# Expert buffers on early-dying tiles, the expert sort behind the first unit, and a product taken by rows, in a two-block transformer kernel

## The chip, the cores and the metric

One core of a Trainium2 chip runs the whole program. The metric is the device time of one launch in microseconds (us); 1440.97 us is the median of three runs of the kernel before.

## The reference

Two residual blocks follow each other on a sequence of 256 tokens of width 1024, all in float32.

- First block: `x + gate1 * mixer(h)`, then `x + gate2 * moe(h)`, and an RMS norm. `h` is an RMS norm of `x`, scaled and shifted by a modulation vector computed from the condition `c` (1024 x 6144 weights, "ada"). The mixer joins a 31-tap causal convolution branch and a chunked linear-attention branch (mLSTM) and ends in a 1024 x 1024 product with `w_out`.
- The MoE picks for each token one of 4 groups, then the best 2 of the 8 experts in that group. Each of the 32 experts is a gated product: `(silu(x Wg) * (x Wu)) Wd`, with 1024 x 512, 1024 x 512 and 512 x 1024 weights, 6 MB an expert, 192 MB in all. The two outputs of a token are added with their routing weights.
- Second block: two layers of differential attention and of grouped-query attention, each with a gated feed-forward of width 2816 and its own modulation.

## The kernel before

**Tiles and engines.** Weights come in as 1 MB tiles `raw` (128 x 2048 float32) through one DMA queue, that of SP, in a fixed order. In the mixer and the second block a weight is split into a high and a low part (`hi` on ACT, `lo` on DVE) and multiplied three times; in the MoE it is multiplied as it is. The tile framework places semaphores and orders each engine's instructions: of those that are ready in its plan, the one written earliest goes first. On the chip each engine then runs its list in that order and waits where it must. `issue_after(ins)` adds to this that what is written in its block, on the engine of `ins`, is issued behind `ins`.

**Space.** Pools lie behind each other in the order in which they are opened, and a closed pool's space goes to the next one opened. The mixer's pools `pha` (its activations), `worka` (`gtmp`, `adarow`, `junk`) and `hia` (split weights) are closed at its end. Then the MoE opens `moe` (its own tiles), `raw2` (3 weight tiles) and `raw3` (5), on the same space. The 8 tiles of `rawp` live through the whole kernel. An expert load waits until every older tile under its buffer is finished with.

**Between mixer and MoE.** `second` multiplies 512 columns of `w_out` for both halves `t` of 128 tokens; `add_gated` adds the product to `x` and `sq_part` squares it (tile `junk`); `norm_rows` makes `xn`, transposes it (`nt`), and `modulated` makes `h32`, of which 16 pieces of 128 x 128 are needed. From it come the 36 routing logits (`plg`), a chain of small DVE instructions from `lg` (L756) to `a01` (L796), and the rank of each token within its expert (`prk`, `sl` L813). `xh` and `xl` are the two parts of `xn`. Modulation work for a later layer stands in a list `queue`, from which `fill` runs steps: 8 loads with their products (`ada`), and a last step that uses the row (`adac`).

**Sort.** `counts` (`cnt`) adds up the tokens of each expert, `place` and `perm` rank the experts, `rows` gives their `order`, and `pst`, `psp`, `swp` bring slots and weights into that order. The first four experts are fixed; the others run in the order found, and `SP` reads `order` before it issues their loads. All of it stands ahead of the first gather.

**Units.** Ten units of 2 or 4 experts: `gather` (every second unit) builds selection matrices `gr` and multiplies them with `xl` and `xh` into `xg`; `gate_up` multiplies `xg` with the weights (`pg`, `pu`) into `hid`; `scatter_of` transposes `gr` (`pG`); `transposed` makes `hT`; `down` multiplies (`pd`), and the unit's `combine` adds into `acc` after the next unit's gate and up. Expert loads are numbered 0 to 191 and rotate over 16 buffers, so load 16 goes where load 0 was: unit 0 has loads 0 to 11. Buffers alternate:

```python
pools["raw"], pools["n"] = [raw2, rawp] * 3 + [raw3, rawp] * 5, 0
```

Ahead of unit 2 stands `fallback`, code for experts with too many tokens: a branch (L853) that every engine meets and that these inputs jump over. After the MoE, `late`, `workb`, `hib` and `xn` are opened on the MoE's space, `rot` and `gqk` are loaded, and the second block begins with `x + acc`, two norms (DVE and ACT) and the first `dense` product.

Of the kernel before, what the change touches and what calls it, by code (L numbers as in the profile page):

```python
# [42 lines left out]
def kernel(ctx: ExitStack, tc: tile.TileContext, I, cst, out):  # L43
# [156 lines left out]
    def ada_steps(key, w, ccol, b0, nb, use):  # L200
# [6 lines left out]
        def step(i):  # L207
            def f():
# [159 lines left out]
    def second(H, w, n0, name, fills=1, kn=KT, n=512):  # L368
        ps = [pa(name) for _ in range(2)]
        for kh in range(kn // 4):  # L370
            wt = split(load_k(w, kh * 4, 4, n0, n))
            for t in range(2):
                for kk in range(4):
                    k = kh * 4 + kk
                    mm3(ps[t][:, :n], (H[0][:, k, t * 128:(t + 1) * 128], H[1][:, k, t * 128:(t + 1) * 128]),
                        wt(kk, 0, n), k == 0, k == kn - 1)
        fill(fills)
        return ps
# [7 lines left out]

    pp = pha.enter_context(tc.tile_pool(name="pha", bufs=1))
# [30 lines left out]
    ca = pp.tile([128, C_PA - C_P], F32, name="ca")  # L418
    SP.dma_start(out=ca, in_=cst[:, C_P:C_PA])
    SP.dma_start(out=bif, in_=I["b_if"].rearrange("o n -> n o"))  # L420
    wif = pp.tile([128, KT, 8], F32, name="wif")
# [8 lines left out]
    wdc = pp.tile([128, 124], F32, name="wdc")  # L430
# [5 lines left out]
    ifg = pp.tile([128, 2, 8], F32, name="ifg")  # L436

    def gates_a():
        wifh = pp.tile([128, KT, 8], F32R, name="wifh")
        ACT.activation(wifh, wif, AF.Copy)  # L440
        wifl = pp.tile([128, KT, 8], F32R, name="wifl")
# [4 lines left out]
        ifr = pp.tile([8, T], F32, name="ifr", tag="ifr")  # L446
# [6 lines left out]
    def gates_b():  # L453
        li, fg = ifg[:, :, 0:4], ifg[:, :, 4:8]
        af = pp.tile([128, 2, 4], F32, name="af")
# [3 lines left out]
        lf = pp.tile([128, 2, 4], F32, name="lf")  # L459
# [5 lines left out]
        bt = pp.tile([128, 2, 4], F32, name="bt")  # L465
        DVE.tensor_copy(bt, pbt)
        rt = pp.tile([128, 2, 4], F32, name="rt")
# [3 lines left out]
    def gates_c(rt, bt):  # L471
# [3 lines left out]
        mx = [pp.tile([4, 128 + T], F32, name=f"mx{i}") for i in range(2)]  # L475
# [11 lines left out]
        en = pp.tile([128, 2, 4], F32, name="en")  # L487
# [24 lines left out]
    lp = pp.tile([64, 2], F32, name="lp")  # L512
# [5 lines left out]
    ls = pp.tile([128, 2], F32, name="ls")  # L518
# [13 lines left out]
    va = pp.tile([128, 2, NH, 129], F32, name="va")  # L532
# [4 lines left out]
    so = pp.tile([128, 2, 512], F32, name="so", tag="so")  # L537
# [4 lines left out]
    mrh = pp.tile([4, T], F32R, name="mrh", tag="ifr")  # L542
    DVE.tensor_copy(mrh, mrow)
    mrl = pp.tile([4, T], F32R, name="mrl")
    sub_lo(mrl, mrow, mrh)
    sel4r = pp.tile([4, 4, 128], F32R, name="sel4r")
    DVE.tensor_copy(sel4r, sel4)
    identr = pp.tile([128, 128], F32R, name="identr")
    DVE.tensor_copy(identr, ident)
    maskr = pp.tile([128, 128], F32R, name="maskr")  # L550
    DVE.tensor_copy(maskr, maskt)
    hm = pp.tile([128, 2, NH, 128], F32, name="hm")
    nums = {}
    for h in range(NH):
# [5 lines left out]
        wT = pp.tile([128, 384], F32, name="wT", bufs=2)  # L560
# [22 lines left out]
    st = pp.tile([128, 8, 6], F32, name="st")  # L583
    mv = pp.tile([128, 8, 2], F32, name="mv")
# [3 lines left out]
    rs = pp.tile([128, 8], F32, name="rs")  # L588
# [45 lines left out]
    sq = pp.tile([128, 4, T], F32, name="sq", tag="so")  # L634
# [43 lines left out]
    for n in range(2):  # L678
        ps = second(M, I["w_out"][0], 512 * n, "wo", 0)
        wo.append(ps)  # L680
# [3 lines left out]
    fill(len(queue))  # L684
# [4 lines left out]
    with tc.tile_pool(name="moe", bufs=1) as pp, \  # L689
            tc.tile_pool(name="raw2", bufs=3) as raw2, tc.tile_pool(name="raw3", bufs=5) as raw3:  # L690
        pools["raw"], pools["n"] = [raw2, rawp] * 3 + [raw3, rawp] * 5, 0
# [3 lines left out]
        def expert_loads():  # L695
            for ne, r0 in UNITS:
                w = ewt[r0] = [{}, {}, {}]
                for r in range(r0, r0 + ne):
                    if r not in at:
                        at[r] = nc.values_load(order[0:1, r:r + 1], engines=[mybir.EngineType.SP], min_val=0, max_val=NE - 1,  # L700
                                               skip_runtime_bounds_check_because="a permutation of the experts")
# [32 lines left out]
        for _ in modulated(nt, AB2, lambda ks, ts: h32[:, ks, ts]):  # L734
            pass
# [3 lines left out]
        for t in range(2):  # L739
            for k in range(KT):  # L740
                mm(plg[:, t, :], h32[:, k, t * 128:(t + 1) * 128], wr[:, k, :], k == 0, k == KT - 1)
        for t in range(2):
            DVE.tensor_copy(xh[:, t, :], xn[:, t, :])
            sub_lo(xl[:, t, :], xn[:, t, :], xh[:, t, :])
# [62 lines left out]
        counts = pc("cnt")  # L807
        for t in range(2):
            mm(counts[0:64, 0:32], ones[:, 0:64], a01[:, t, :], t == 0, t == 1)
        for d in range(2):  # L810
            for t in range(2):
                mm(counts[32 * d:32 * d + 32, 32:33], a01[:, t, :], ones[:, 0:1], t == 0, t == 1)
        DVE.scalar_tensor_tensor(sl, prk, 1.0, a01, op0=ALU.add, op1=ALU.mult)  # L813


        scratch2 = pp.tile([128, 512], F32, name="scratch2", tag="yl", bufs=2)
        kb = tl([64, 33], "kb")
        DVE.tensor_tensor(kb, counts[0:64, 0:33], km[0:64, 0:33], ALU.add)
        cnt = tl([64, 1], "cnt")
        DVE.tensor_copy(cnt, counts[0:64, 32:33])  # L820
        above = tl([64, 32], "above")
        DVE.tensor_scalar(above, kb[:, 0:32], kb[:, 32:33], None, op0=ALU.is_gt)
        place = pp.tile([64, 1], F32, name="place")
        DVE.tensor_reduce(place, above, axis=AX, op=ALU.add)
        perm = scratch2[0:64, 0:64]
        DVE.tensor_scalar(perm, iota[0:64], place, km[0:64, 34:35], op0=ALU.subtract, op1=ALU.is_equal)
        rows = pb("rows")
        mm(rows[0:1, 0:32], km[0:32, 33:34], perm[0:32, 0:32])
        mm(rows[0:1, 32:64], cnt[0:32], perm[0:32, 0:32])
        order = pp.tile([1, 32], I32, name="order")  # L830
        DVE.tensor_copy(order, rows[0:1, 0:32])
        excess = scratch2[0:1, 320:352]
        DVE.tensor_tensor(excess, rows[0:1, 32:64], km[0:1, 35:67], ALU.subtract)
        mx1 = tl([1, 1], "mx1")
        DVE.tensor_reduce(mx1, excess, axis=AX, op=ALU.max)
        ovi = pp.tile([1, 1], I32, name="ovi")
        DVE.tensor_scalar(ovi, mx1, 0.5, None, op0=ALU.is_gt)
        pst = pb("pst")
        for t in range(2):
            PE.transpose(pst[0:64, t * 128:(t + 1) * 128], sw[:, t, :], ident)  # L840
        swT = scratch2[0:64, 64:320]
        DVE.tensor_copy(swT, pst[0:64, 0:256])
        psp = pb("psp")
        for t in range(2):
            mm(psp[:, t * 64:(t + 1) * 64], swT[:, t * 128:(t + 1) * 128], perm)
        swp = pp.tile([128, 2, 64], F32, name="swp")
        DVE.tensor_copy(swp, psp[:, 0:128].rearrange("p (t n) -> p t n", t=2))
        slp, wEp = swp[:, :, 0:32], swp[:, :, 32:64]

        def fallback():  # L850
            over = nc.values_load(ovi, min_val=0, max_val=1,
                                  skip_runtime_bounds_check_because="a comparison gives zero or one")
            with tc.If(over > 0, preferred_fallthrough_block=False):  # L853
                wide = pp.tile([64, 33], F32, name="wide")
                DVE.tensor_scalar(wide[:, 32:33], place, WIDE - 0.5, float(CAP4), op0=ALU.is_lt, op1=ALU.mult)
# [37 lines left out]
        def gather(u):  # L893

            ne, r0 = UNITS[u]
            cap = 128 // ne
            src = sl if r0 < FIXED else slp
            gr = pp.tile([128, 2, 256], F32R, name="gr", bufs=2)
            for t in range(2):
                DVE.tensor_tensor(gr[:, t].rearrange("p (e s) -> p e s", s=cap),  # L900
                                  iota[:, None, 0:cap].to_broadcast([128, 2 * ne, cap]),
                                  src[:, t, r0:r0 + 2 * ne].unsqueeze(2).to_broadcast([128, 2 * ne, cap]), ALU.is_equal)
            xg = pp.tile([128, KT, 256], F32, name="xg", tag="xg", bufs=2)
            for k2 in range(KT // 2):
                ps = pb("gath")
                for j in range(2):
                    k = 2 * k2 + j
                    o = ps[:, j * 256:(j + 1) * 256]
                    for t in range(2):
                        mm(o, xl[:, t, k * 128:(k + 1) * 128], gr[:, t, :], t == 0, False)  # L910
                        mm(o, xh[:, t, k * 128:(k + 1) * 128], gr[:, t, :], False, t == 1)
# [533 lines left out]
```

## Time and profile before

| | |
|---|---|
| median of 3 runs | 1440.97 us (1440.58 to 1442.58) |
| the profiled execution's own time | 1442.87 us |
| its span, first to last instruction | 1441.1 us |
| mean granted TensorE clock | 0.965 |
| busy share of the span | PE 90%, DVE 43%, ACT 34%, POOL 4% |

The span is cut into four parts by eye: start and mixer to about 261 us, routing to about 290 us, the units to about 746 us, and the second block. Times in rows are us from the span's start. PE is TensorE, PEld its weight loads, DVE VectorE, ACT ScalarE, POOL GpSimd, SP SyncE; a q behind a name is the engine's sequencer. A PE product of float32 operands shows as two instructions.

### The profile page before, as it was taken

How to read it: one execution, taken by the hardware profiler on the slowest of the kernel's cores; microseconds unless marked ns; L12 is line 12 of the kernel's file. 1: busy time of each engine (PE TensorE's matmuls, PEld its weight loads, DVE VectorE, ACT ScalarE, POOL GpSimd, SP SyncE). 2: the span in 40 equal slices, each digit the busy share in tenths (PEclk: the TensorE clock that was granted, in tenths of full speed). 3: DMA queues.
4: the chain of work that ended last, by engine and by line, in shares of the span. 5: the costliest groups of instructions: out<-in, count | busy, mean ns of one | idle time of the engine just before them, and what ended most of it. 6: DMA issues, size and time to landing. Idle time of an engine off the chain costs nothing.

```text
span 1441.1 us, 20075 instructions
## 1 busy us (share of the span) xinstructions
PE 1292.9 (90%) x8125; PEld 889.5 (62%) x8125; DVE 620.7 (43%) x1074; ACT 491.0 (34%) x840; POOL 58.0 (4%) x99
## 2 busy tenths in 40 slices
PE   5799999897997777677769999999999999999997
PEld 1686897644342222121117876698999777799997
DVE  0799857511111011010026545754444764744454
ACT  1465354311010000010025645643442554644442
POOL 0000000000000000000002220000000120000000
PEclk9899999798999999899998999999999999999999
DMA  8987557798899999999989666757554665855500
GB/s 303 403 287 258 196 193 264 305 415 374 375 426 425 426 425 426 426 426 425 426 347 366 225 216 224 261 185 273 172 194 144 223 226 195 297 185 176 175 30 30
DMA packets 142658, 408.83 MB, mean 284 GB/s; under 512 B 10057, under 2 KB 90430, under 8 KB 111842
## 3 DMA queue, kind: packets, MB, share of 16 engines
q1 hardware_dynamic: 142562, 407.51, 74.2%
q8 instruction: 65, 1.06, 0.3%
q14 instruction: 31, 0.25, 0.0%
HBM read 406.43 MB, written 1.05 MB: 283 GB/s over the span
## 4 chain that ended last, share of the span: by engine, by line
PE 67%; DMA 25%; DVE 3%; issue 2%; ACT 1%; POOL 1%; SPq 0%; POOLq 0%; DVEq 0%; ACTq 0%
DMA raw<-experts_dram 23%; PE ada L124 6%; PE fg L120 3%; PE fu L119 3%; PE fg L119 3%; PE fg L121 3%; PE fu L120 3%; PE fu L121 3%; PE facc L119 3%; PE facc L120 3%; PE facc L121 3%; PE pd L124 2%; PE dense L119 2%; PE dense L120 2%; PE dense L121 2%; PE pu L124 2%
## 5 line engine op out<-in xcount | busy, mean ns | idle before, releaser
L92 DVE TENSOR_TENSOR lo<-raw,hi 128x1024 fp32r<-128x1024 f32 x120 | 145.2, 1230 | 127.3 <-ACT hi L90 125.0
L110 DVE TENSOR_TENSOR lo<-raw,hi 128x1024 fp32r<-128x1024 f32 x120 | 146.2, 1224 | 95.6 <-ACT hi L108 95.3
L90 ACT ACTIVATE hi<-raw 128x1024 fp32r<-128x1024 f32 x120 | 125.1, 1061 | 145.0 <-PE facc L121 79.1
L108 ACT ACTIVATE hi<-raw 128x1024 fp32r<-128x1024 f32 x120 | 125.9, 1057 | 122.3 <-issue 55.8
L124 PE MATMUL pu<-raw,xg 128*32 128x512 f32 (+1 forms) x512 | 108.7, 638 | 29.8 <-DMA raw<-experts_dram 29.8
L124 PE MATMUL pg<-raw,xg 128*32 128x512 f32 (+1 forms) x512 | 117.5, 690 | 17.5 <-DMA raw<-experts_dram 17.5
L124 PE MATMUL pd<-raw,hT 128*32 128x512 f32 (+1 forms) x512 | 113.5, 597 | 16.0 <-DMA raw<-experts_dram 8.3
L124 PE MATMUL ada<-raw,cc 128*32 128x512 f32 x576 | 98.6, 638 | 7.2 <-DMA raw<-in_w_ada_dram 6.4
L928 DVE TENSOR_TENSOR hid<-hid,pu 128x256 f32<-128x256 f32 x20 | 7.5, 418 | 226.1 <-PE pu L124 226.1
L119 PE MATMUL fg<-Hh,lo 128*128 128x256 f32 x352 | 100.7, 286 | 4.3 <-DVE Hh L351 4.3
L120 PE MATMUL fg<-Hl,hi 128*128 128x256 f32 x352 | 100.8, 286 | 0.9 <-DVE Hl L115 0.9
L121 PE MATMUL fg<-Hh,hi 128*128 128x256 f32 x352 | 100.5, 286 | 0.0
L119 PE MATMUL fu<-Hh,lo 128*128 128x256 f32 x352 | 100.5, 285 | 0.0
L120 PE MATMUL fu<-Hl,hi 128*128 128x256 f32 x352 | 100.0, 284 | 0.0
L121 PE MATMUL fu<-Hh,hi 128*128 128x256 f32 x352 | 99.9, 284 | 0.0
L124 PEld LDWEIGHTS pu<-raw,xg 128*32 128x32 f32 (+1 forms) x512 | 28.2, 123 | 98.5 <-DMA raw<-experts_dram 53.7
L124 PEld LDWEIGHTS pd<-raw,hT 128*32 128x32 f32 (+1 forms) x512 | 31.1, 116 | 84.6 <-issue 58.5
L119 PE MATMUL dense<-hi,Hl 128*128 128x256 f32 x288 | 82.9, 288 | 0.0
L120 PE MATMUL dense<-lo,Hh 128*128 128x256 f32 x288 | 81.5, 283 | 0.0
L121 PE MATMUL dense<-hi,Hh 128*128 128x256 f32 x288 | 81.4, 284 | 0.0
L124 PEld LDWEIGHTS pg<-raw,xg 128*32 128x32 f32 (+1 forms) x512 | 28.1, 129 | 82.4 <-issue 46.5
L966 DVE SCALAR_TENSOR_TENSOR pd<-pd,ws,gate 128x512 f32<-128x512 f32 x20 | 15.2, 759 | 133.1 <-PE pd L124 132.1
(413 smaller groups left out, 2665.1 us busy)
## 6 DMA issues: line engine op xcount, KB each, us to landing
raw<-experts_dram SPq DMA_DIRECT2D x192, 1024.0 KB
raw<-in_ada_w_dram SPq DMA_DIRECT2D x48, 1024.0 KB
raw<-in_f_w_in_dram SPq DMA_DIRECT2D x44, 1024.0 KB
raw<-in_w_ada_dram SPq DMA_DIRECT2D x24, 1024.0 KB
raw<-in_f_w_out_dram SPq DMA_DIRECT2D x22, 1024.0 KB
raw<-in_w_in_dram SPq DMA_DIRECT2D x20, 1024.0 KB
raw<-in_a_w_qkv_dram SPq DMA_DIRECT2D x12, 1024.0 KB
raw<-in_b_w_qkv_dram SPq DMA_DIRECT2D x6, 1024.0 KB
```

The costliest lines, as they stand in the source:

```text
L90: ACT.activation(hv, src, AF.Copy)
L92: DVE.tensor_tensor(lv, src, hv.bitcast(F32), ALU.subtract)
L108: ACT.activation(hv, src, AF.Copy)
L110: DVE.tensor_tensor(lv, src, hv.bitcast(F32), ALU.subtract)
L119: PE.matmul(o, al, bh, start=first, stop=False, skip_group_check=True)
L120: PE.matmul(o, ah, bl, start=False, stop=False, skip_group_check=True)
L121: PE.matmul(o, ah, bh, start=False, stop=last, skip_group_check=True)
L124: return PE.matmul(o, a, b, start=first, stop=last, skip_group_check=True)
L928: DVE.tensor_tensor(hid[:, c], hid[:, c], pgu[1][:, c], ALU.mult)
L966: DVE.scalar_tensor_tensor(pd, pd, ws, gate2[:, n * 512:(n + 1) * 512], op0=ALU.mult, op1=ALU.mult)
```

## The change

- The mixer's tiles are divided into `p1` (`pha1`: 28.5 KB a partition, all that is finished with before the last products) and `pp` (`pha`: `upad`/`ah`, `t8` for `sga` and `sgb`, `uacc`/`al`, 33.5 KB). `p1` is opened first. The MoE opens `raw2` and `raw3` first and `moe` behind them, and the ring of 16 becomes 3 of `raw2`, 2 of `rawp`, 5 of `raw3`, 6 of `rawp`.
- The last `w_out` product runs all of token half 0 first, then half 1.
- Of `h32`, DVE makes the upper four pieces of both halves (before: of half 1 alone). `xh` and `xl` are queued behind DVE's last piece.
- The modulation row's last step (`adarow`, `adac`) is one step `end`; that of the next layer is issued behind the last logit product, followed by three products that nothing reads (`warm`).
- The first gather stands right behind `sl`. The sort becomes a function, whose PE work is queued behind the last `up` product of unit 0, together with that unit's `scatter_of`; loads 24 to 27 are written behind it.

```diff
-                if i == n - 1:
-                    st["a"] = pools["work"].tile([128, 512], F32, name="adarow")
-                    ACT.copy(st["a"], ps)
             return f
-        return [step(i) for i in range(n)] + [lambda: use(st["a"])]
+        def end():
+            a = pools["work"].tile([128, 512], F32, name="adarow", **pools.get("adarow", {}))
+            ACT.copy(a, st["ps"])
+            use(a)
+        return [step(i) for i in range(n)] + [end]
...
-    def modulated(banks, AB, dst):
+    def modulated(banks, AB, dst, share=lambda ks, ts: ks.start and ts.start):
...
-                if ks.start and ts.start:
-                    DVE.tensor_scalar(d[:, j, :], src, A, B, op0=ALU.mult, op1=ALU.add)
+                if share(ks, ts):
+                    chain["mod"] = DVE.tensor_scalar(d[:, j, :], src, A, B, op0=ALU.mult, op1=ALU.add).ins
...
+        for kh, t in ((0, 0), (1, 0), (0, 1), (1, 1)) if rows_first else ((0, 0), (0, 1), (1, 0), (1, 1)):
+            if kh not in wts:
+                wts[kh] = split(load_k(w, kh * 4, 4, n0, 512))
...
+    p1 = pha.enter_context(tc.tile_pool(name="pha1", bufs=1))
     pp = pha.enter_context(tc.tile_pool(name="pha", bufs=1))
...
-        ps = second(M, I["w_out"][0], 512 * n, "wo", 0)
+        ps = second(M, I["w_out"][0], 512 * n, "wo", 0, n == 1)
...
-    fill(len(queue))
+    fill(len(queue) - 1)
...
-    with tc.tile_pool(name="moe", bufs=1) as pp, \
-            tc.tile_pool(name="raw2", bufs=3) as raw2, tc.tile_pool(name="raw3", bufs=5) as raw3:
-        pools["raw"], pools["n"] = [raw2, rawp] * 3 + [raw3, rawp] * 5, 0
+    with tc.tile_pool(name="raw2", bufs=3) as raw2, tc.tile_pool(name="raw3", bufs=5) as raw3, \
+            tc.tile_pool(name="moe", bufs=1) as pp:
+        pools["raw"], pools["n"] = [raw2] * 3 + [rawp] * 2 + [raw3] * 5 + [rawp] * 6, 0
...
-        for _ in modulated(nt, AB2, lambda ks, ts: h32[:, ks, ts]):
+        for _ in modulated(nt, AB2, lambda ks, ts: h32[:, ks, ts], lambda ks, ts: ks.start):
             pass
...
-        for t in range(2):
-            DVE.tensor_copy(xh[:, t, :], xn[:, t, :])
-            sub_lo(xl[:, t, :], xn[:, t, :], xh[:, t, :])
+        with tc.issue_after(end.ins):
+            pools["work"], pools["adarow"] = pp, {"tag": "yh", "bufs": 2}
+            fill(len(queue))
+            pools.pop("adarow")
+            warm = pc("warm")
+            for _ in range(3):
+                mm(warm, ones, cs[:, 0:512])
+        with tc.issue_after(chain["mod"]):
+            for t in range(2):
+                DVE.tensor_copy(xh[:, t, :], xn[:, t, :])
+                sub_lo(xl[:, t, :], xn[:, t, :], xh[:, t, :])
...
+        gathered = gather(0)
+        def sort():
+            counts = pc("cnt")
...
-            load_to(done + RAW_BUFS + RAW2_BUFS)
+            load_to(24 if u == 0 else done + RAW_BUFS + RAW2_BUFS)
             if u % 2 == 0:
-                gr, xg = gather(u)
+                gr, xg, _ = gather(u) if u else gathered
...
-            gT, ws = scatter_of(ne, r0, gr[:, :, g])
+            with tc.issue_after(chain["up"]) if u == 0 else nullcontext():
+                if u == 0:
+                    sort()
+                    load_to(done + RAW_BUFS + RAW2_BUFS)
+                gT, ws = scatter_of(ne, r0, gr[:, :, g])
```

## Rows read from the trace of the kernel before

**Rows 1.** The page's busy times: us (share of the span) xinstructions.

```profile
PE 1292.9 (90%) x8125; PEld 889.5 (62%) x8125; DVE 620.7 (43%) x1074; ACT 491.0 (34%) x840; POOL 58.0 (4%) x99
```

**Rows 2.** Busy time by stretch: length, engines' busy us (instructions), PE clock, DMA share, GB/s.

```profile
240.00:264.00 24.00, 24.00 (x122) 17.38 (x120) 12.45 (x17) 8.10 (x13) 0.93 (x1) 1.00 0.52 188
...
356.00:364.00 8.00, 8.00 (x39) 4.35 (x40) 0.76 (x2) 2.89 (x6) 0.00 (x0) 0.87 0.07 24
364.00:742.00 378.00, 297.17 (x1520) 93.46 (x1516) 37.71 (x84) 26.79 (x54) 0.00 (x0) 0.95 1.01 425
```

**Rows 3.** Timeline, expert loads issued by SP: start, us, instruction; loads 4 to 19; 16; 40.

```profile
262.02 37.26 SPq L69 DMA_DIRECT2D raw<-experts_dram  x16
...
294.67 0.33 SPq L69 DMA_DIRECT2D raw<-experts_dram  x1
...
362.91 0.34 SPq L69 DMA_DIRECT2D raw<-experts_dram  x1
```

**Rows 4.** Timeline from the mixer's last sum to the first gather.

```profile
261.61 0.69 DVE L383 TENSOR_TENSOR x<-x,gtmp 128x512 f32<-128x512 f32 x1
...
264.82 1.46 POOL L309 TENSOR_TENSOR rstd<-ms,half 128x1 f32<-128x1 f32 x1 [2.12 <-DVE ms L314]
...
271.52 0.23 DVE L756 TENSOR_TENSOR scratch<-plg,brt 128x72 f32<-128x72 f32 x1 [1.17 <-PE plg L124]
...
276.22 0.42 PE L124 MATMUL prk<-scratch,cs 128*128 128x32 f32 x1 [4.74 <-DVE scratch L796]
...
277.63 0.64 PE L124 MATMUL cnt<-scratch,ones 128*64 128x32 f32 x4
277.74 0.23 DVE L813 SCALAR_TENSOR_TENSOR sw<-prk,scratch 128x64 f32<-128x64 f32 x1 [0.84 <-PE prk L124]
...
278.82 0.41 DVE L900 TENSOR_TENSOR gr<-cs,sw 128x256 fp32r<-128x256 f32 x1
...
283.15 1.12 PE L124 MATMUL psp<-scratch 64*128 64x64 f32 x4
...
284.20 0.58 PE L124 MATMUL gath<-gr,xl 128*128 128x256 f32 x1
```

**Rows 5.** Groups on DVE, 260.7 to 272 us: count, busy us, mean ns.

```profile
L115 DVE TENSOR_TENSOR xl<-xn,xh 128x1024 fp32r<-128x1024 f32 x2 | 2.4, 1220 | 0.0
L743 DVE CAST xh<-xn 128x1024 fp32r<-128x1024 f32 x2 | 1.4, 690 | 1.6 <-ACT xn L322 1.6
L342 DVE TENSOR_SCALAR h<-nt,AB 128x128 f32<-128x128 f32 x4 | 1.4, 402 | 0.0
L324 DVE TENSOR_SCALAR xn<-x,rstd 128x1024 f32<-128x1024 f32 x1 | 0.8, 753 | 0.4 <-POOL rstd L309 0.4
```

**Rows 6.** Stretches of 4 us around the gather; the third number from the right is PE's clock.

```profile
272.00:276.00 4.00, 0.00 (x0) 0.00 (x0) 3.62 (x21) 0.98 (x5) 0.00 (x0) 0.59 1.01 422
...
288.00:292.00 4.00, 4.00 (x20) 2.82 (x21) 0.06 (x1) 2.28 (x6) 0.00 (x0) 0.78 1.01 426
```

**Rows 7.** Timeline of PE between the first unit's up and down products.

```profile
304.33 1.45 PE L124 MATMUL pu<-raw,xg 128*64 128x512 f32 x4
...
308.25 0.65 PE L124 MATMUL pd<-raw,hT 128*64 128x512 f32 x2 [0.83 <-issue]
```

**Rows 8.** The branch over the fallback: count, ns least/median/most, first and last start.

```profile
L853 PEldq COMPARE_BRANCH x2: 95/3120/6144, 345.4 to 345.7; - x2
```

**Rows 9.** Groups of ACT, 749 to 760 us.

```profile
L90 ACT ACTIVATE hi<-raw 128x1024 fp32r<-128x1024 f32 x3 | 3.1, 1040 | 0.0
L305 ACT ACTIVATE junk<-x 128x512 bf16<-128x512 f32 x4 | 2.5, 622 | 2.2 <-DMA raw<-in_a_w_qkv_dram 2.2
```

**Rows 10.** Instructions of `rot`'s load (L1006), then the chain that ended last from 749 us.

```profile
L1006 SPq EVENT_SEMAPHORE  x4: 17/28/8693, 739.2 to 739.4; - x4
...
750.78 9.08 DMA raw<-in_ada_w_dram
```

**Rows 11.** Groups of PE, 200 to 216 us: four float32 products of 256 columns.

```profile
L124 PE MATMUL lnm<-uacc,ones 128*128 128x256 f32 x8 | 1.9, 378 | 0.0
```

More of the change, by code (lines that the diff above doesn't have):

```diff
@@ L474, in gates_c @@
             PE.transpose(prow[0:4, t * 128:(t + 1) * 128], rt[:, t, :], ident)
-        mx = [pp.tile([4, 128 + T], F32, name=f"mx{i}") for i in range(2)]
+        mx = [p1.tile([4, 128 + T], F32, name=f"mx{i}") for i in range(2)]
         for i in range(2):
@@ L740 @@
             for k in range(KT):
-                mm(plg[:, t, :], h32[:, k, t * 128:(t + 1) * 128], wr[:, k, :], k == 0, k == KT - 1)
-        for t in range(2):
-            DVE.tensor_copy(xh[:, t, :], xn[:, t, :])
-            sub_lo(xl[:, t, :], xn[:, t, :], xh[:, t, :])
+                end = mm(plg[:, t, :], h32[:, k, t * 128:(t + 1) * 128], wr[:, k, :], k == 0, k == KT - 1)
+        with tc.issue_after(end.ins):
[9 more added lines that the diff above has]
+                sub_lo(xl[:, t, :], xn[:, t, :], xh[:, t, :])
         scratch = pp.tile([128, 512], F32, name="scratch", tag="yh", bufs=2)
@@ L817 @@
[L817 to L847, printed above, removed]
@@ new lines @@
+        gathered = gather(0)
+        by = {}
+        def sort():
+            counts = pc("cnt")
+            for t in range(2):
+                mm(counts[0:64, 0:32], ones[:, 0:64], a01[:, t, :], t == 0, t == 1)
+            for d in range(2):
+                for t in range(2):
+                    mm(counts[32 * d:32 * d + 32, 32:33], a01[:, t, :], ones[:, 0:1], t == 0, t == 1)
+            scratch2 = pp.tile([128, 512], F32, name="scratch2", tag="yl", bufs=2)
+            kb = tl([64, 33], "kb")
+            DVE.tensor_tensor(kb, counts[0:64, 0:33], km[0:64, 0:33], ALU.add)
+            cnt = tl([64, 1], "cnt")
+            DVE.tensor_copy(cnt, counts[0:64, 32:33])
+            above = tl([64, 32], "above")
+            DVE.tensor_scalar(above, kb[:, 0:32], kb[:, 32:33], None, op0=ALU.is_gt)
+            place = by["place"] = pp.tile([64, 1], F32, name="place")
+            DVE.tensor_reduce(place, above, axis=AX, op=ALU.add)
+            perm = scratch2[0:64, 0:64]
+            DVE.tensor_scalar(perm, iota[0:64], place, km[0:64, 34:35], op0=ALU.subtract, op1=ALU.is_equal)
+            rows = pb("rows")
+            mm(rows[0:1, 0:32], km[0:32, 33:34], perm[0:32, 0:32])
+            mm(rows[0:1, 32:64], cnt[0:32], perm[0:32, 0:32])
+            order = by["order"] = pp.tile([1, 32], I32, name="order")
+            DVE.tensor_copy(order, rows[0:1, 0:32])
+            excess = scratch2[0:1, 320:352]
+            DVE.tensor_tensor(excess, rows[0:1, 32:64], km[0:1, 35:67], ALU.subtract)
+            mx1 = tl([1, 1], "mx1")
+            DVE.tensor_reduce(mx1, excess, axis=AX, op=ALU.max)
+            ovi = by["ovi"] = pp.tile([1, 1], I32, name="ovi")
+            DVE.tensor_scalar(ovi, mx1, 0.5, None, op0=ALU.is_gt)
+            pst = pb("pst")
+            for t in range(2):
+                PE.transpose(pst[0:64, t * 128:(t + 1) * 128], sw[:, t, :], ident)
+            swT = scratch2[0:64, 64:320]
+            DVE.tensor_copy(swT, pst[0:64, 0:256])
+            psp = pb("psp")
+            for t in range(2):
+                mm(psp[:, t * 64:(t + 1) * 64], swT[:, t * 128:(t + 1) * 128], perm)
+            swp = pp.tile([128, 2, 64], F32, name="swp")
+            DVE.tensor_copy(swp, psp[:, 0:128].rearrange("p (t n) -> p t n", t=2))
+            by["slots"], by["weights"] = swp[:, :, 0:32], swp[:, :, 32:64]
@@ L891 @@
         acc = [pa("acc") for _ in range(4)]
[L893 to L911, printed above, removed]
-                    ACT.activation(xg[:, k, :], o, AF.Identity, scale=AB2[:, 0, k:k + 1], bias=AB2[:, 1, k:k + 1])
-            return gr, xg
         def gate_up(ne, w, xe):
@@ L932, in scatter_of @@
             cap = 128 // ne
-            src = wE if r0 < FIXED else wEp
+            src = wE if r0 < FIXED else by["weights"]
             g2 = [g[:, t, :].bitcast(F32) for t in range(2)]
```

105 lines of the change are left out of this document (58 added, 47 removed).

## The prediction

> **What bounds the kernel now.** I read the busy times first, then stretches of the span, then the timeline of the places that the edits touch, and last the chain that ended last. PE is busy for 90% of the span [rows 1], but that is a mean over stages with different limits. From 364 to 742 us DMA moves 425 GB/s with a share of 1.01, while PE is busy for 297 of 378 us [rows 2]: there the expert loads set the time, and only an earlier start of that stream ends it earlier. The stream has two holes ahead of it: 188 GB/s in 240 to 264 us, before the first unit, and 24 GB/s in 356 to 364 us, after the second [rows 2]. So the first question is what ends each hole.
>
> The first hole: only loads 0 to 3 are issued by 262.02 us, when the next 16 (loads 4 to 19) start [rows 3]. Against 425 GB/s the stretch lost (425 - 188) / 425 x 24 = 13.4 us of transfer. But the ring has 16 buffers. Load 16 waits for unit 0 to finish with load 0's buffer, and this is so at 294.67 us [rows 3]. From here I call that moment r.
>
> The second hole: load 40 goes out at 362.91 us [rows 3], r + 68.24. It waits for the first gate product of unit 2, and so for PE's list: unit 0, unit 1, the branch over the fallback, the second gather. PE's second branch instruction takes 6.14 us [rows 8], in which PE does nothing. By transfer alone 24 loads (16 to 39) of 1.05 MB at 425 GB/s need 59.2 us, so PE's list, not the stream, sets when load 40 goes. What counts is when r comes and how long PE takes from r to load 40.
>
> **The change part by part.** The sum has five terms.
>
> *Buffers on early tiles.* By the sizes in the code the three `raw2` tiles take bytes 0 to 24,576 of a partition and lie wholly on the vectors read at the start and on `p1`. Four `raw3` tiles reach into `sga`, `sgb` and `al`, which end with the last mixer sums; the fifth reaches into `junk`. So 8 loads no longer wait for the weight splits of `w_out`, and most of the 13.4 us of lost transfer comes back. Yet the 16 loads of the ring are 16 x 2.47 = 39.5 us of transfer; started by 240 us they are there by about 280 us, ahead of r. Then the stream stops until r. I cost this at zero. The cover is the ring's size; with more buffers it would be worth up to 13.4 us.
>
> *Term 1, r.* (a) From the mixer's end to `lg`. The last sum of `x` ends at 262.30 us [rows 4], unchanged: taking the last product by rows ends half 0 earlier, but its `xn` lies on `gtmp` and `junk` now and waits for half 1's sum and square all the same. The square follows at once (0.62 us, [rows 9]), `rstd` takes the 1.46 us of [rows 4], `xn` 0.75 us, and DVE then has eight pieces of `h32` at about 0.34 us, 1.4 us for four [rows 5]. With the hand-overs they end near 268.2 us. Then come `xh` and `xl`, two of each, 1.4 + 2.4 = 3.8 us [rows 5], and two short instructions of the moved modulation step, together some 0.3 us by the 0.23 us of a short one [rows 4]. These are written ahead of `lg` and ready at once, so I take them to be issued ahead of it: `lg` at 272.4 us, 0.9 us later than the 271.52 us of [rows 4]. If `lg` went first, it would stand near 269.3 us, 2.2 us earlier. (b) From `lg` to the gather, before: 284.20 - 271.52 = 12.68 us [rows 4]. After: 4.70 us to the first rank product, 1.52 us to `sl`, then `sl` (0.23 us), one selection matrix `gr` (0.41 us) and a hand-over, in all about 7.0 us [rows 4]. That is 5.7 us less. (c) From the gather to r: 294.67 - 284.20 = 10.47 us [rows 3, 4]. PE ran at half clock in it until the middle of 288 to 292 us (0.78 there, 0.59 in 272 to 276 us, where it had nothing to do, [rows 6]), about 5.6 us. After, PE has the modulation products and `warm` behind the logits, then 4 us of nothing until the ranks. I expect the low clock to begin later and to last some 4 us of the gather: 0.8 us less, between 0 and 2.8 us (all of the 5.6 us at full clock). Together r moves by 0.9 - 5.7 - 0.8 = -5.6 us.
>
> [...]
>
> *Term 2, the sort in unit 0's gap.* Before, PE goes from the last `up` (305.78 us) to the first `down` (308.25 us) in 2.47 us [rows 7]; that is `hid`, its transposes and `hT`. Now the counts, the transposes of the weights, the ranked products and unit 0's `pG` are written ahead of those transposes, and the sort's DVE instructions ahead of `hT`. As filler between dependent steps they cost PE about 2 us and DVE about 2.5 us. I take 2.2 us. Bounds: 1 us, when all but the counts hide in the waits that are there anyway, and 8.1 us, the sort in series as before, from 277.63 us to the end of `psp` at 284.27 us [rows 4], with `pG`, an estimate of 1.5 us by the 0.64 us of four small products [rows 4]. Behind it waits `down`, thus the buffers of loads 8 to 11, thus loads 24 to 27, and on SP everything behind them. SP reads `order` for load 24, which the sort gives well ahead of that buffer. The whole delay lies on PE's list, so it moves load 40 one for one.
>
> *Term 3, PE before the branch.* It stands idle for those 6.14 us at the branch [rows 8], and the clock falls there too. The second gather may meet another phase of it: -0.6 us, between -1.2 and 0.
>
> *Term 4, the end of the units.* SP waits 8.69 us at `rot` [rows 10], whose place lies on MoE tiles that die last; the second block's next weight loads are queued behind it, and the chain then waits 9.08 us for one of them [rows 10]. After, `rot`, `junk` and the split tiles lie on weight buffers of the last unit's gate and up, which are free before. So these loads go at least 8.7 us earlier. Next late is the chain of squares and norms: ACT's first square waits 2.2 us, and three splits of 1.04 us stand among the eight squares [rows 9]. With room for the split tiles I expect the first two splits ahead of the chain: -2.0 us. Bounds: -0.3 us (the splits stay where they are) and -3.8 us (all three go, and 0.7 us of the wait).
>
> *Term 5, the rest: zero.* Loads on `raw2` that now run among those of `w_out` delay these by at most 3 x 2.47 = 7.4 us of transfer; PE is busy for all of 240 to 264 us [rows 2], so those loads were there in time, and I leave the 7.4 us as the price if they weren't early enough. The second weight split of the last product is needed earlier, at about 252 us; its first part is there. `warm` (2.8 us by four products of half its width, 1.9 us, [rows 11]) runs while PE waits for the routing. The new ring order moves which buffers are free at the end: two of `rawp` early, six with the last down products, all ahead of the 748 us at which SP gets past `rot` now (739.4 + 8.69, [rows 10]).
>
> Sum: -5.6 + 2.2 - 0.6 - 2.0 = -6.0 us. In the profiled execution (span 1441.1, own time 1442.87) that gives 1436.9 us. It lies 1.9 us above the median of 1440.97, against which I forecast 1435.0 us.
>
> **The rivals.** *A. The routing goes ahead of the copies,* and `lg` comes 2.2 us before its old time in place of 0.9 us after it. The gather meets the low clock earlier, with much the same loss. Then the sum is 3.1 us lower, with a little from the clock 3.8: 1431.2 us. For it speaks that DVE has holes between the routing's short instructions; against it the order in which things are written.
>
> *B. The sort runs in series ahead of the first `down`:* term 2 is 8.1 us, the sum -0.1 us, 1440.9 us. For it speaks that each of its steps needs the one before; against it that PE can do the transposes of `hid` in between.
>
> *C. The same place decides the other sign.* If SP, or `hT`, comes behind the whole sort and the load of `order` as well, `down` starts later still. Above 8.2 us the delay eats everything gained; from 11.1 us on the kernel is slower by over 0.2%. With 12 us it would be 1444.8 us. Against it: the serial sort took 6.6 us, at half clock.
>
> *D. The earlier fill is worth its 13.4 us,* because r is not what load 16 waits for: with terms 3 and 4 the time is about 1425 us. Against it stands that the ring gives load 16 load 0's buffer, whose products come behind the first gather, whatever was loaded early.
>
> *E. The change doesn't do what it says,* since PE is the busiest engine. PE's work isn't less, and `warm` adds 2.8 us: 1441.0 to 1443.8 us. [...]
>
> **How the numbers follow.** What a measurement can tell from no change is about 0.2%, 2.9 us: same is 1438.1 to 1443.9 us. The forecast's case has 0.52 (its own range 1430.5 to 1439.5 us: r between -7.6 and -4.3, term 2 between 1 and 3.5 us, terms 3 and 4 between their bounds, not all at one end), A 0.16, B 0.14, C 0.07, D 0.05, E 0.06. Faster: all of A and D and 0.46 of the forecast's, 0.67. Same: B, E and 0.06, 0.26. Slower: C, 0.07. The range goes from 1428.5 us (A with the better bounds) to 1440.5 us (short of most of B and E). It leaves out D, C and about half of B and E, with some of the forecast's ends: 2 in 10.
>
> **What would show it.** In the profile of the changed kernel: expert loads in 214 to 240 us and DMA near 425 GB/s from 240 to about 275 us, then a hole until r; load 16 near 289 us; the first gather within 1 us of `sl`; `lg` right behind the last `xl`; 4 to 5 us between unit 0's last `up` and first `down`; load 40 near 359 us; no SP wait at `rot`. The prediction is wrong if `lg` stands ahead of the copies, if the sort takes more than 5 us of PE's list, or if load 40 isn't set by PE.

## The result, and the profile after

The changed kernel takes 1449.45 us (median of 5 runs, 1448.62 to 1450.59) against 1440.97 us (5 runs, 1439.85 to 1442.58): ratio 1.0051, 95% interval [1.0035, 1.0067]. It is slower by 7.3 us by the ratio (the two medians lie 8.5 us apart), where 6 us less were forecast, and lies above the range. Its profiled execution has a span of 1447.8 us, 6.7 us more than that of the execution that [rows 1] come from.

The engines are as busy as in [rows 1], so their sums over the span don't tell where the time went:

```profile
PE 1299.2 (90%) x8131; PEld 892.6 (62%) x8131; DVE 622.5 (43%) x1078; ACT 489.8 (34%) x836; POOL 56.9 (4%) x99
```

So I cut the span at points that both kernels have, and took each stretch as the difference of two times in the kernel's own timeline (us; the last two columns are experiments told below):

| stretch | before | after | modulation step late | sort among the gates |
|---|---|---|---|---|
| start to the mixer's last product | 260.84 | 261.07 | 259.14 | 259.67 |
| to the first gather product | 23.36 | 20.35 | 17.68 | 17.67 |
| to unit 0's last up product | 21.58 | 20.55 | 20.60 | 23.98 |
| to the first down product | 2.47 | 5.82 | 7.04 | 2.29 |
| to the issue of load 40 | 54.66 | 55.51 | 55.60 | 53.12 |
| to the last down product | 382.95 | 382.71 | 382.66 | 382.49 |
| to the second block's first dense product | 19.04 | 17.65 | 17.65 | 17.63 |
| to the end of its first layer's last product | 357.20 | 357.91 | 358.06 | 357.65 |
| to the end of its second layer's last product | 311.69 | 318.99 | 313.15 | 311.50 |

The reader is to see two things. Up to the last line but one, the change saves 0.5 us in all, where the sum had 6.0. And then 7.3 us are lost in the second block's second layer, where no line of the diff names anything.

**The loss.** Timeline of PE in that layer, changed kernel (start, us, engine, line, operation; in brackets the idle time before it and what ended it):

```profile
1192.00 0.39 PE L119 MATMUL oacc<-hi,oTl 128*128 128x512 f32 x1
1193.66 0.74 PE L124 MATMUL adag<-gtmp,selrr 32*128 32x512 f32 x4 [1.27 <-DVE gtmp L115]
```

Stretches of the same layer (columns as in [rows 2]; the third number from the right is PE's clock), the last one of the kernel before:

```profile
1180.00:1192.00 12.00, 12.00 (x77) 9.02 (x78) 7.97 (x19) 7.44 (x23) 2.63 (x3) 1.00 0.66 213
1192.00:1205.00 13.00, 11.72 (x40) 7.58 (x38) 5.96 (x10) 3.77 (x5) 0.30 (x1) 0.61 0.56 184
```
```profile
1192.00:1205.00 13.00, 12.96 (x69) 7.92 (x68) 7.92 (x18) 5.99 (x14) 0.20 (x1) 1.00 0.30 90
```

PE stands 1.27 us before the products that spread a gate row (`adag`), and behind that it runs at half clock until 1205 us (0.50 in 1195 to 1204 us): 40 instructions in 13 us, where the kernel before gets 69 done in the same 13 us at a clock of 1.00. The mean of 0.61 is 10.2 of the 13 us at the low level (13 x (1 - 0.61) / 0.5 is 10.1), so by estimate it costs 5.1 us; with the wait that is 6.4 us. The layer as a whole gives a little less. Run 3's kernel below, without this wait, takes 313.15 us there for 318.99 us, which is 5.8 us; both have a low stretch of 3.4 us at about 1125 us (in the changed kernel 0.57 in 1126 to 1130 us) that the kernel before does not have, and the other 1.5 of the 7.3 us go with it. What PE waits for stands on DVE (its timeline):

```profile
1189.11 1.12 DVE L1285 SCALAR_TENSOR_TENSOR tok<-dense,ss,gqk 128x128 f32<-128x128 f32 x4 [0.74 <-POOL ss L1280]
...
1190.74 0.96 DVE L1293 TENSOR_TENSOR rope<-tok,rot 128x256 f32<-128x256 f32 x1
1191.63 0.95 DVE L1295 TENSOR_TENSOR rotated<-rope 128x256 f32<-128x256 f32 x1
1192.50 0.41 DVE L1296 TENSOR_TENSOR rotated<-rope 128x256 f32<-128x256 f32 x1
1192.84 0.68 DVE L115 TENSOR_TENSOR gtmp<-adarow,gtmp 128x512 fp32r<-128x512 f32 x1
```

The subtraction that makes `gtmp` is queued behind the rotation of a query pair. In the kernel before it stands ahead of that rotation; and ACT, whose copy of the row (`adarow`) it needs, makes that copy 2.84 us later now (timelines: DVE before, ACT before, ACT after):

```profile
1186.97 0.69 DVE L115 TENSOR_TENSOR gtmp<-adarow,gtmp 128x512 fp32r<-128x512 f32 x1 [2.59 <-ACT gtmp L242]
```
```profile
1184.06 0.59 ACT L227 COPY adarow<-ada 128x512 f32<-128x512 f32 x1
```
```profile
1186.90 0.62 ACT L229 COPY adarow<-ada 128x512 f32<-128x512 f32 x1
```

The step `end` copies the row only when it is called, one `fill` later than the last products of the row; the planner then puts what needs the copy later on each engine's list. The edit was made for the moved step, but `ada_steps` serves all of them.

**The routing.** Timeline of the changed kernel, DVE first, PE behind it:

```profile
268.32 0.68 DVE L756 CAST xh<-xn 128x1024 fp32r<-128x1024 f32 x1
271.93 0.17 DVE L258 SCALAR_TENSOR_TENSOR AB<-adac,vc 128x8 f32<-128x8 f32 x1 [2.93 <-PE adac L124]
...
273.82 0.22 DVE L769 TENSOR_TENSOR scratch<-plg,brt 128x72 f32<-128x72 f32 x1
273.96 1.21 DVE L115 TENSOR_TENSOR xl<-xn,xh 128x1024 fp32r<-128x1024 f32 x1
275.10 0.15 DVE L773 TENSOR_REDUCE scratch<-scratch 128x2 f32<-128x8 f32 x1
```
```profile
270.05 1.85 PE L124 MATMUL adac<-cs,adarow 128*128 128x4 f32 x8
271.75 5.23 PE L124 MATMUL warm<-cs,ones 128*128 128x512 f32 x6
279.51 0.41 PE L124 MATMUL prk<-scratch,cs 128*128 128x32 f32 x2 [2.52 <-DVE scratch L809]
...
281.42 0.55 PE L124 MATMUL gath<-gr,xl 128*128 128x256 f32 x1 [0.87 <-DVE gr L829]
```

DVE stands 2.93 us in the middle of the copies: the modulation step's `AB` is queued there, and its products `adac` stand on PE behind the logits. `lg` (L769) is at 273.82 us against 271.52 [rows 4], with one `xl` of 1.21 us between it and the first maximum. The gather is 2.8 us earlier than in [rows 4] and load 16 goes out 3.0 us earlier than in [rows 3] (SP's timeline, loads 16 and 40):

```profile
291.69 0.80 SPq L69 DMA_DIRECT2D raw<-experts_dram  x2
...
363.30 0.34 SPq L69 DMA_DIRECT2D raw<-experts_dram  x1
```

Load 40 is 0.4 us later than in [rows 3], though. One place between takes it back, the sort (timeline of PE between unit 0's up and down, to be held against [rows 7]):

```profile
301.80 0.37 PE L124 MATMUL cnt<-scratch,ones 128*64 128x32 f32 x4
...
303.17 0.41 PE L955 MATMUL pG<-cs,gr 128*128 128x128 f32 x2 [0.77 <-DVE scratch L860]
...
304.65 0.21 PE L124 MATMUL rows<-scratch,km 32*1 32x32 f32 x2 [0.73 <-DVE scratch L866]
...
305.76 0.66 PE L124 MATMUL psp<-scratch 64*128 64x64 f32 x4
306.35 0.66 PE L970 MATMUL pT<-cs,hid 128*128 128x128 f32 x4
307.79 1.12 PE L124 MATMUL pd<-raw,hT 128*64 128x512 f32 x2 [0.78 <-DVE hT L971]
```

The transposes of `hid` come last in the list, not between the sort's steps, so the gap is 5.82 us. And the clock falls on its far side (307 to 312 us, 0.66), so that the 32 `pd` behind it take 8.54 us in place of 7.09 us.

**The loads.** The early fill is there (stretches to be held against [rows 2]):

```profile
240.00:264.00 24.00, 24.00 (x119) 17.57 (x121) 12.99 (x18) 8.12 (x14) 0.87 (x2) 1.00 0.68 273
356.00:364.00 8.00, 8.00 (x39) 4.63 (x39) 0.76 (x2) 3.17 (x6) 0.00 (x0) 0.84 0.00 1
364.00:742.00 378.00, 296.32 (x1522) 94.06 (x1518) 37.68 (x84) 26.79 (x54) 0.00 (x0) 0.95 1.01 425
742.00:766.00 24.00, 14.79 (x84) 7.20 (x85) 16.03 (x31) 15.76 (x35) 2.54 (x4) 0.86 1.05 402
```

273 in place of 188 GB/s ahead of 264 us, not the 425 that I expected: seven loads went out by 253 us. Behind them SP's list has two other loads, `gf` and `km`; by SP's waits the first stood 9.0 us for the last use of `gate1`, the second 1.1 us for the last square into `junk`, and the next nine expert loads, queued behind both, went out from 263.75 us on. The hole at 356 us is as empty as it was.

### The profile page after: what moved, and what is told of

It is laid out like the page before. It is cut to its first block, busy times and chain, and to the rows that moved or that the text cites. A ratio compares the mean times of both kernels' runs of the same rounds, so it can differ in the third digit from the quotient of the medians.

```text
span 1447.8 us, 20067 instructions
## 1 busy us (share of the span) xinstructions
PE 1299.2 (90%) x8131; PEld 892.6 (62%) x8131; DVE 622.5 (43%) x1078; ACT 489.8 (34%) x836; POOL 56.9 (4%) x99
## 4 chain that ended last, share of the span: by engine, by line
PE 48%; DMA 22%; DVE 2%; issue 2%; ACT 1%; POOL 1%; POOLq 0%; SPq 0%; DVEq 0%; ACTq 0%
DMA raw<-experts_dram 22%; PE ada L124 3%; PE fu L119 3%; PE fg L120 3%; PE fu L120 3%; PE fu L121 3%; PE fg L119 3%; PE fg L121 3%; PE facc L119 3%; PE facc L120 3%; PE facc L121 3%; PE dense L119 2%; PE dense L120 2%; PE dense L121 2%; PE pd L124 2%
## 5 line engine op out<-in xcount | busy, mean ns | idle before, releaser
L124 PE MATMUL pg<-raw,xg 128*32 128x512 f32 (+1 forms) x512 | 110.8, 654 | 17.9 <-DMA raw<-experts_dram 17.9
```

Of the source, the lines that this page charges most:

```text
L124: return PE.matmul(o, a, b, start=first, stop=last, skip_group_check=True)
```

## The experiments

All were timed against the kernel before, in 9 to 12 runs each; the runs of before in the three sets have medians of 1441.91, 1442.06 and 1441.91 us.

**1. The row steps apart** on the changed kernel:

```diff
+                if i == n - 1 and not joined:   # joined: the moved step alone
+                    row()                       # the copy, as before
...
```

> The changed kernel, but each modulation step copies its row in its last products again, with the use of the row as a step of its own; only the step that the change moved behind the logits keeps both in one. Theory 1 (the joined step is the loss): PE no longer stands 1.27 us before the second block's last gate products (adag) and keeps full clock behind them, so 1.27 + 5.1 = 6.4 us come back, 1443.1 us, and the low stretch at 1194.8 us is gone. Theory 2 (the low clock came from the other edits having moved the work by some us, and would fall there anyway): only the wait of 1.27 us comes back, 1448.2 us.

1443.16 us, ratio 1.0006 [0.9993, 1.0018]: theory 1. The list of PE in that layer is again that of before, product for product, and there is no wait at `adag` and no low stretch at 1194 us.

**2. The joined step alone** on the kernel before:

> The kernel before with one edit alone: copy and use of a modulation row joined in one step. Theory 1: the same wait before adag and the same 10 us of low clock appear near 1193 us, 1440.97 + 6.4 = 1447.4 us. Theory 2: the wait alone, 1442.2 us, or no change.

1446.17 us, ratio 1.0035 [1.0019, 1.0051], which is 5.0 us (2.7 to 7.4). Theory 1 again: PE waits 1.26 us before `adag`, and the clock falls, for 6.8 us here and not for 10 (two stretches, columns as above):

```profile
1190.00:1194.00 4.00, 2.74 (x17) 1.87 (x17) 4.00 (x6) 2.13 (x3) 0.57 (x1) 1.00 0.44 178
1194.00:1201.00 7.00, 7.00 (x22) 4.42 (x21) 2.15 (x6) 1.64 (x2) 0.00 (x0) 0.51 0.65 182
```

**3. One row put back** (`joined = not (key == 2 and b0 == 4)`) on the changed kernel:

> The changed kernel with one row copy put back: only the second block's last step with gate products (adag near 1190 us) copies its row in its last products again; all other steps stay joined. Theory (this one step's place on ACT, and with it that of its subtraction on DVE, makes PE's wait and the low stretch behind it): all of the 6.4 us come back, 1443.1 us as with all steps apart. Rival (the steps lose a little each): most of the loss stays, 1446 us or more.

1442.71 us, ratio 1.0003 [0.9990, 1.0015]. One ACT copy of 0.62 us, called one `fill` earlier, gives 6.7 us back (the difference of two medians from different sets of runs). PE's timeline:

```profile
1187.25 0.40 PE L121 MATMUL oacc<-hi,oTh 128*128 128x512 f32 x1
1187.58 0.74 PE L124 MATMUL adag<-gtmp,selrr 32*128 32x512 f32 x4
```

And the stretch that had lost:

```profile
1192.00:1205.00 13.00, 13.00 (x71) 8.08 (x70) 7.19 (x17) 5.98 (x14) 0.00 (x0) 1.00 0.35 102
```

**4. The buffers alone** on the kernel before (pools and ring of the change, nothing else):

> The kernel before with the buffers alone changed: the expert buffers on the early mixer tiles, the matching order of the ring. Theory 1 (the ring of 16 caps what an early fill is worth; only the end of the units gains): 1.4 us less, 1439.6 us, load 16 within 0.5 us of its old 294.67 us. Rival (the early fill is worth its transfer): 13.4 us less, 1427.6 us. Rival (loads among those of the last mixer weights delay these): up to 7.4 us more, 1448 us.

1445.93 us, ratio 1.0028 [1.0015, 1.0041]: a miss of all three expectations. Load 4 goes out at 242.37 us, but load 16 at 298.20 us, later than before, with the gather (26.49 us from the mixer's last product in place of 23.36). DVE and ACT both stand for `adac` (timelines, POOL's last instruction ahead of it first, ACT's last):

```profile
264.21 0.54 POOL L309 TENSOR_TENSOR rstd<-ms,half 128x1 f32<-128x1 f32 x1 [0.74 <-DVE ms L314]
...
266.98 0.17 DVE L256 SCALAR_TENSOR_TENSOR AB<-adac,vc 128x8 f32<-128x8 f32 x1 [2.85 <-PE adac L124]
...
267.14 0.75 DVE L324 TENSOR_SCALAR xn<-x,rstd 128x1024 f32<-128x1024 f32 x1
```
```profile
267.06 1.15 ACT L322 ACTIVATE xn<-x,rstd 128x1024 f32<-128x1024 f32 x1 [1.23 <-PE adac L124]
```

`rstd` is ready at 264.75 us, and `xn` reads nothing of `adac`; but it lies on the space of the modulation row now and has to let the row's last use go first. So the new space goes with the moved step, and the moved step made the edit of `end`. That load 16 followed the gather and not the fill does bear out the ring.

**5. The modulation step late:** steps apart as in 1, and the moved step behind the first gather.

```diff
+        with tc.issue_after(gathered[2]):   # was: behind the last logit product
+            pools["work"], pools["adarow"] = pp, {"tag": "yl", "bufs": 2}
+            fill(len(queue))
...
```

> As the run with the steps apart, and the moved modulation step goes behind the first gather in place of behind the logits. Theory (DVE stood 2.93 us behind the logits for this step's products, with both splits of x and the routing queued behind it): the first split's end, 272.2 us, sets the routing's start, the first maximum comes at 272.5 us in place of 275.10 us, the gather and load 40 come 2.6 us earlier: 1440.5 us. Rival (the gather meets more of the low clock, or PE's list behind it eats it): 1442 to 1443.5 us, load 40 still near 363 us.

1441.97 us, ratio 1.0004 [0.9990, 1.0018], 1.2 us under run 1, which the intervals don't tell apart. By the traces the routing did what the theory says: run 1 has 20.08 us from the mixer's last product to the gather, this one 17.68 us, 2.4 us less. But between up and down it has 7.04 us (run 1: 5.83), and the low clock falls there (stretches). Four kernels with the sort at this place bear it out: their gaps are 5.83, 6.14, 6.47 and 7.04 us, with 0.3, 1.5, 2.3 and 3.7 us of low clock in them (runs 1, 6, 7, 5).

```profile
298.00:302.00 4.00, 2.64 (x21) 2.51 (x21) 2.89 (x15) 0.00 (x0) 0.00 (x0) 0.85 1.01 424
302.00:308.00 6.00, 5.21 (x17) 2.30 (x19) 2.64 (x10) 0.00 (x0) 0.00 (x0) 0.53 1.02 431
```

**6. The old space** on run 5's kernel:

> As the run with the modulation step behind the gather, with the pools and the ring's order of the kernel before, so that the expert loads wait for the mixer's end again (load 4 near 262 us in place of 240 us). Theory (16 buffers are full ahead of load 16 either way): load 16 and load 40 within 0.5 us of the same distance from the mixer's end; only the 0.3 us at the end of the units are lost, 1442.3 us. Rival (the early fill is worth its 13.4 us of transfer): 1455 us. Rival (the new space costs something elsewhere, such as the low stretch near 1125 us that the kernel before does not have): 1440.3 us.

1442.37 us, ratio 1.0001 [0.9988, 1.0014]. From the first gather to load 40 it takes 83.39 us, with the new space 83.24 us (20.60 + 7.04 + 55.60). Load 4 goes out 21.5 us later, counted from the mixer's last product, and the time does not show it, as the theory has it (1442.3 us).

**7. Without `warm`** on run 5's kernel (the three products left out; nothing reads them):

> As the run with the modulation step behind the gather, without the three products that only keep PE working (warm). Theory (the low stretch comes whether they run or not, and the ranks don't wait for them): within 1 us, 1441 to 1443 us, the first gather at the same distance from the mixer's end. Rival (activity keeps the clock): without them more of the gather runs at half clock, up to 2.8 us more, 1444.8 us.

1439.94 us, ratio 0.9992 [0.9980, 1.0004]. The gather to the last up takes 20.99 us, with `warm` 20.60 us: 0.4 us, not 2.8. The time lies below both forecasts, and its interval doesn't tell it from run 5.

**8. The sort behind the first down** on run 5's kernel:

> As the run with the modulation step behind the gather, and the sort goes behind the last down product of the first unit in place of behind its last up product. Theory (the sort in series costs PE 3.35 us between up and down, and up to 3.5 us more where the low clock falls on it): up to down takes 2.9 us or less again in place of 7.04 us; the sort's products stand among the first combine and the second unit's gates and cost at most 2 us there; load 40 is 2 to 4 us earlier, 1439 us. Rival (the same steps stand in series at the new place, or the expert loads that need the sort come late): nothing won, 1442 us or more.

1446.1 us, ratio 1.0028 [1.0017, 1.0039]: the rival, which had 1442 us or more. Up to down is 2.23 us, as it was before, but now `down` to load 40 takes 61.97 us in place of 55.60 us. The same steps stand in series at the new place, with the first combine, which otherwise stands behind the second unit's products, among them (timeline of PE):

```profile
310.75 0.37 PE L124 MATMUL cnt<-scratch,ones 128*64 128x32 f32 x4
...
312.40 0.50 PE L124 MATMUL acc<-yl,gT 128*128 128x512 f32 x1 [1.05 <-DVE yl L115]
...
315.27 0.80 PE L124 MATMUL acc<-yl,gT 128*128 128x512 f32 x1 [1.11 <-DVE yl L115]
...
318.13 1.11 PE L124 MATMUL psp<-scratch 64*128 64x64 f32 x4
319.18 1.12 PE L124 MATMUL pg<-raw,xg 128*64 128x512 f32 x2
```

**9. The sort among the gates** on run 7's kernel: `sort` becomes a generator of three stages.

```diff
+                    if stages and (h, i) != (1, 1):
+                        with tc.issue_after(chain["up"]):
+                            next(stages)   # counts | rows, pst | psp
...
```

> As the run without the warm products (steps apart, modulation step behind the gather), with the sort in three stages behind the first unit's gate and up products, 16 products between stage and stage, so that DVE's part of each runs while PE works. Theory (the sort's price was its series of hand-overs between PE and DVE, not its products): up to down takes 2.5 to 3 us in place of 6.47 us, load 40 comes 3.5 us earlier, 1436.4 us. Rival (the loads take it back, because the stream of the later units ends when it did): load 40 earlier, the end of the units within 1 us of where it was, 1439.5 us.

1439.0 us, ratio 0.9978 [0.9968, 0.9988]: 0.2% faster than the kernel before, and faster than the changed one. Up to down is 2.29 us; among the gates the stages cost PE their products alone, with no wait before any of them (timeline of PE):

```profile
287.85 0.37 PE L124 MATMUL cnt<-scratch,ones 128*64 128x32 f32 x4
...
288.37 3.65 PE L124 MATMUL pu<-raw,xg 128*64 128x512 f32 x16
291.96 0.21 PE L124 MATMUL rows<-scratch,km 32*1 32x32 f32 x2
...
297.08 0.66 PE L124 MATMUL psp<-scratch 64*128 64x64 f32 x4
297.66 3.65 PE L124 MATMUL pu<-raw,xg 128*64 128x512 f32 x16
```

From the mixer's last product on, its load 40 is 3.3 us and its last down product 3.7 us earlier than in run 7 (97.06 against 100.39, and 479.55 against 483.29 us), which is what the theory says; but the median moved by 0.9 us only, the ratio by 0.0014, and the time lies near the rival's 1439.5 us, not at the theory's 1436.4 us. And most of the 3.3 us is clock. PE from 300 to 320 us, run 7 first:

```profile
300.00:320.00 20.00, 18.33 (x84) 7.79 (x86) 7.84 (x25) 1.19 (x2) 0.00 (x0) 0.83 0.89 367
```
```profile
300.00:320.00 20.00, 19.78 (x102) 7.45 (x99) 6.20 (x15) 1.19 (x2) 0.00 (x0) 1.00 1.01 427
```

Run 7 has a low stretch of 6.8 us there, run 9 none. Of the 3.3 us, 2.1 lie behind the first `down` product, where the two lists are alike; and 0.6 of the other 1.2 us is what the low clock adds to run 7's gap (6.47 us for run 1's 5.83). So the sort's waits themselves account for some 0.6 us. The rest goes with them all the same: in each of the seven kernels that have the sort's steps in one gap (the changed one, runs 1, 3 and 5 to 8) a low stretch of 3.4 to 6.8 us falls in that gap or right behind it, between 300 and 322 us, and the five others have none from 293 to 341 us.

**10. The same with the old space:**

> The same as the run with the sort among the gates, with the pools and the ring's order of the kernel before. Theory (the early fill is worth nothing while the ring of 16 waits for the first unit): within 1 us of that run. Rival (with r this early, the late start of the loads shows: 16 x 2.47 us from 262 us on end at 301.5 us): the first unit waits for its loads and it is 2 us or more slower.

1438.01 us, ratio 0.9970 [0.9957, 0.9983], not to be told from run 9. The first unit does not wait for its loads: the gather to the last up takes 23.82 us, with the new space 23.98 us. By the trace load 40 is 1.2 us later from the mixer's last product on (98.27 against 97.06 us), with a low stretch of 10.2 us around the branch in place of 6.8 us. Even with the sort hidden, the times show no gain from the early fill.

## Why the prediction was wrong

**The step that failed is term 5, "the rest: zero".** Of the edit of `end` it priced the moved step alone (two short instructions, in term 1). The same function makes every other modulation row, and for one of them the later copy costs 5.0 us by run 2, 6.7 us by run 3's median and 5.8 us by its trace. Within the intervals that is the distance from before to after. Without it the change is worth nothing measurable (runs 1 and 3), so the 6.0 us were not there either: up to that layer the stretches give -3.0 us (r), -0.8 (from r to unit 0's last up product, 10.28 for 11.11 us, in no term), +3.35 (the sort), +0.85 (to load 40), -0.2 (to the last down product), -1.4 (the end of the units) and +0.7 (the first layer, in no term and not explained by a run), together -0.5 us. None of the rivals had this place. The sentence on what would make the prediction wrong named three signs, and none of them is what did it.

The other terms, from the stretches:

- **Term 1.** r is 3.0 us earlier for 5.6. (a) `lg` was to be 0.9 us later and is 2.3 us later. The short instructions were priced by their durations (0.3 us); the wait that one of them brings, on `adac` behind the logits, is 2.93 us with the copies and the routing queued behind it. That it is `adac` run 5 shows: moved away, the gather comes 2.4 us earlier. (b) Selection ahead of the counts did what was said: 7.60 us from `lg` to the gather for 12.68, which is 5.1 us less for 5.7, as the second `xl` stands in it. (c) 10.27 us from the gather to r for 10.47: -0.2 for -0.8 us, since the low stretch came later (280.0 to 286.9 us) and covers 5.5 us of it, as it covered 5.6 us before.
- **Term 2.** +3.35 us for +2.2. Of this the sort's own products are about 1.6 us (what they add among the gates in run 9, where no wait comes with them); most of the rest is waits in the hand-overs between PE and DVE, 0.77 and 0.73 us in the timeline above. The size was off because the transposes of `hid` stood behind the sort's steps and filled none of these waits. Rival B's 8.1 us was not reached. Behind `down` (run 8) the same steps cost more.
- **Term 3.** The branch did what was said: from unit 1's last down to the second gather 11.85 us for 12.28. But the clock fell at another place that the sum did not have, the first `down` (1.45 us), so that the stretch to load 40 is +0.85 us in place of -0.6 us. By what run 9 shows, this fall comes with the sort in its gap: it is a part of the sort's price that term 2 left out.
- **Term 4.** -1.4 us for -2.0 us, inside its bounds. SP waits 2.0 us at `rot` for 8.69, DMA moves 402 GB/s in 742 to 766 us for 305, and ACT's first square waits 1.45 us for 2.2; but the splits stayed among the squares, for which the prediction had -0.3 us. That -1.4 us lies inside the bounds is luck in part. What the new space is worth depends on the clock: with it the stretch takes 17.6 us whether the low stretch in it is 6.8 us long (the changed kernel) or 10.2 us (runs 3 and 9); with the old space it is 17.9 us at 6.8 us (runs 2 and 10) and 19.0 and 19.5 us at 10.2 us (before, run 6). So 0.3 to 1.8 us.
- **The early fill at zero** was right (runs 6 and 10), and rival D is out. The hole at 356 us ends when PE's list gets there: load 40 goes out 4.50 us behind the start of unit 2's first gate product in the kernel before and 4.51 us in the changed one.
- **The clock.** Behind the wait at `adag` it fell in both kernels that have the wait (for 10.2 us in the changed one, 6.8 us in run 2's) and in none of the others. But waits of 1.7 us (`pT`, at about 1157 us) and 1.2 us (`oT`, at about 1179 us), which all twelve traces have in that layer, are followed by no fall in any, so how long PE stood doesn't decide it alone. What does stays open; and as the later copy also reorders PE's list there, wait and new order were never tried apart.

On `warm`: in the changed kernel it ran at half clock from 271.75 us (0.54 in 272 to 277 us; 5.23 us for six instructions, 2.8 us in run 5's), and the gather met a low stretch all the same (280.0 to 286.9 us; 0.50 in 282 to 286 us). Had `warm` held the clock for the gather, as run 7's rival has it, leaving it out would cost up to 2.8 us; run 7 has 0.4 us. But PE stood again behind `warm`, 2.5 us in the changed kernel and 3.7 us in run 5's, so what the runs decide against is such a filler ahead of a further wait; one with no wait behind it was not tried.

Open as well: the last stretch of the table is 311.1 to 313.2 us in kernels with one and the same list of PE there. The five at 313.1 to 313.2 us (runs 1, 3, 4, 5, 10) have a low stretch of 3.4 us between 1119 and 1133 us, the other five don't. It begins some 0.2 us or less behind the end of a wait of 0.9 us (`nt`) that all of them have, so the same list with the same wait can have it or not. It comes with either space, so I count it to neither.

## What to carry to other kernels

An edit in a helper is an edit at each of its calls: list the calls, and price the one with the least slack, not the one it was made for. A small instruction on an engine that runs its list in order is priced by what it waits for, with all that is queued behind it (0.17 us for `AB`, and 2.93 us of waiting). Dependent steps between two engines want stretches of other work of their length between them (among the gates, up to down took 2.29 us in run 9); in one gap they cost their waits, in both gaps tried here (up to down 5.8 to 7.0 us in runs 1, 5, 6 and 7; `down` to load 40 61.97 us in run 8, 55.60 us in run 5), and a low stretch of the clock came with them.

## What the runs showed of the hardware

A wait of 1.27 us on PE was followed by 10.2 us at half clock (0.50 in 1195 to 1204 us): by the estimate of 6.4 us the price was five times the wait's length. A series of waits of 0.7 to 1.1 us in one gap was met by a low stretch in seven kernels of seven (3.4 to 6.8 us; 0.66 in 307 to 312 us in the changed one). Where such stretches fall moves with the list: putting the gather 2.4 us earlier put a low stretch of 6.8 us on the sort's gap (run 5) and gave back half of the gain.
